# One decoder layer on one core: down projection moved into a Strassen stage of its own, activations through DRAM

## The chip, the core and the metric

The kernel is one program for one core of a Trainium2 chip. Five engines run side by side, each with an instruction queue of its own that it works off in order: PE (TensorE, matrix products), DVE (VectorE), ACT (ScalarE), POOL (GpSimd) and SP (SyncE, which issues nearly all DMAs here). An instruction waits at the head of its queue until the semaphores it names are reached, and everything behind it on that engine waits too. The metric is device time in microseconds (us), the median of the runs shown.

## What is computed

One layer: a mixer, a cross attention over 256 memory tokens, and a feed-forward block, then a final norm, for 1024 tokens of width 1024 in float32. The change lies in the feed-forward block and the norm behind it:

```python
def conv_ffn(h, w_up, conv_w, conv_b, w_down):
    u = h @ w_up                       # 1024 x 1024 @ 1024 x 5632
    u_pad = jnp.pad(u, ((0, 0), (CONV_WIDTH - 1, 0), (0, 0)))
    u = conv_b + conv_w[0] * u_pad[:, 0:s] + conv_w[1] * u_pad[:, 1:1 + s] + conv_w[2] * u_pad[:, 2:2 + s]
    gate = u[..., :D_FF]               # D_FF = 2816
    val = u[..., D_FF:]
    return (jax.nn.silu(gate) * val) @ w_down
...
        x = x + conv_ffn(h, ffn_w_up[l], ffn_conv_w[l], ffn_conv_b[l], ffn_w_down[l])
    return rms_norm(x, norm_final_w)
```

## The kernel before

A float32 value is held as a pair hi + lo, each part in the type float32r (`Pair`). A product of two pairs is three matrix instructions, hi*hi, hi*lo, lo*hi (`mm3`, lines 90 to 92). To make a pair from a plain tile costs one ACT copy that rounds to hi and one DVE subtraction for lo (`split`, lines 96 and 97; for weights `wunit`, lines 117 and 118). "Splitting" a tile below means these two instructions.

The feed-forward block works feature by feature: 22 tiles `f` of 128 gate features and the 128 value features that belong to them. The up projection of a tile is cut in 2 x 2 blocks (gate and value columns by halves of k, halves of k by halves of the 1024 tokens) and done with Strassen's seven products in Winograd's form (`up_strassen`), each product 4 k-steps of three matrix instructions of 512 columns: 84 instructions a tile. The sums of weight blocks are made on POOL (lines 919, 920, 925, 929), and the sums of activation blocks once, before the stage (`sums`, `sums3`, with `whole` on POOL at line 801, `less` on DVE at line 805; the results are the tiles `TT[1]` to `TT[4]`). The first two feature tiles (`up_plain`) are done without Strassen, 96 instructions each, since their products need no `TT`. Every product ends in its own PSUM bank, and DVE adds the seven results together (line 948); then come the convolution (`conv`, ACT line 858, DVE lines 859 and 860), SiLU and product (`swiglu`), and the result is split into the pair `gs[f, b]`.

The down projection runs between the up products (`down(part)`): two feature tiles against 512 output columns, for each of 8 token tiles, 6 instructions of 512 columns, and DVE adds the bank to the residual `xres` (line 1020). It is the plain product, 22 x 2 x 8 x 3 = 1056 instructions. The last four feature tiles are done a token tile at a time with the final norm behind each (`down_norm`, line 998 adds, line 299 norms).

The order of the work: `Job`s hold generators that emit a few instructions at a time; `fill` interleaves them with chains of other work. A scheduler then orders each engine's instructions, except those given to `pin`. Weights come as one stream, two units ahead (`Stream`). Buffers decide when loads may start: `big` has 40 slots of 4 KB a partition, `wts` two raw weight buffers (`wraw`) and four split ones (`whi`, `wlo`), `wsum` one more raw buffer and two for sums.

## Time and profile before

| | us |
|---|---|
| three runs | 1334.48, 1337.21, 1338.45 |
| median | 1337.21 |
| span of the profiled execution, first to last instruction | 1335.7 |
| PE busy in it | 1309.3 |
| DVE busy | 935.5 |
| ACT busy | 572.1 |
| POOL busy | 200.8 |

The feed-forward block takes the second half of the span: its first up products start at 634 us and its last ends near 1328 us. The time of the profiled execution is not listed apart from its span; the median lies 1.5 us above the span. A row of the profile that groups instructions names line, engine, operation, what is written and read (`wl<-ws,wh`: the tile `wl` from `ws` and `wh`; names that begin with `p` are PSUM banks), then count, busy time and mean duration.

### The profile page before, as it was taken

What the parts mean: (1) busy time and instruction counts of PE and PEld (TensorE: products, weight loads), DVE (VectorE), ACT (ScalarE), POOL (GpSimd) and SP (SyncE); (2) the same over time, 40 slices, a digit from 0 to 9 for tenths busy, and PEclk for the clock granted to TensorE, in tenths of its full rate; (3) what the DMA queues carried; (4) which work ended last, traced back from release to release, by engine and by line L of the source; (5) the groups of instructions that cost most, each with busy time, mean ns of one, the idle gap of its engine ahead of it and who ended that gap; (6) DMA issues with size and microseconds to landing.
All of it is one profiled execution on the core that took longest, in us unless ns stands there. A gap on an engine that the chain in (4) does not pass through costs nothing.

```text
span 1335.7 us, 17253 instructions
## 1 busy us (share of the span) xinstructions
PE 1309.3 (98%) x6482; PEld 1091.4 (82%) x6482; DVE 935.5 (70%) x1620; ACT 572.1 (43%) x1041; POOL 200.8 (15%) x252
## 2 busy tenths in 40 slices
PE   8999999999999999999889999999999999999997
PEld 7898878988788898989678888888888888888886
DVE  6723775237667554466997988787979788887984
ACT  6536443364445433344352534242433434342542
POOL 2000110001210000021731211202111212112201
PEclk9999999999999999999999999999999999999999
DMA  9333225332332222212112112121212111121122
GB/s 284 139 96 80 78 91 195 95 79 64 96 131 58 64 64 76 84 63 79 32 32 64 48 48 71 40 74 38 63 32 63 48 48 48 49 76 35 33 94 111
DMA packets 125172, 102.29 MB, mean 77 GB/s; under 512 B 3161, under 2 KB 108319, under 8 KB 125088
## 3 DMA queue, kind: packets, MB, share of 16 engines
q1 hardware_dynamic: 124511, 99.35, 24.1%
q0 software_dynamic: 432, 1.57, 0.3%
q8 instruction: 51, 0.84, 0.3%
...
## 4 chain that ended last, share of the span: by engine, by line
PE 87%; DVE 6%; issue 3%; POOL 2%; ACT 1%; DMA 1%; POOLq 0%; SPq 0%; ACTq 0%; DVEq 0%
PE pa L90 21%; PE pa L92 21%; PE pa L91 21%; PE pb L90 6%; PE pb L91 6%; PE pb L92 6%; DVE r L97 2%; PE pb L307 1%; DVE t L805 1%; DVE f L299 1%; DVE wl L118 1%; POOL s L294 1%; PE pb L650 1%; PE pb L760 1%; PE pb L634 1%
## 5 line engine op out<-in xcount | busy, mean ns | idle before, releaser
L117 ACT ACTIVATE wh<-wr 128x512 fp32r<-128x512 f32 (+1 forms) x264 | 166.1, 631 | 360.1 <-PE pa L92 146.4
L92 PE MATMUL pa<-r,wl 128*128 128x512 f32 (+1 forms) x780 | 302.6, 388 | 7.2 <-DVE wl L118 7.2
L90 PE MATMUL pa<-r,wh 128*128 128x512 f32 (+1 forms) x780 | 308.3, 395 | 0.7 <-ACT r L96 0.7
L118 DVE TENSOR_TENSOR wl<-wr,wh 128x512 fp32r<-128x512 f32 (+1 forms) x264 | 195.2, 740 | 158.7 <-ACT wh L117 153.9
L91 PE MATMUL pa<-r,wh 128*128 128x512 f32 (+1 forms) x780 | 302.0, 387 | 2.4 <-DVE r L97 2.4
L90 PE MATMUL pa<-wh,r 128*128 128x512 f32 (+2 forms) x680 | 238.2, 351 | 0.6 <-ACT r L96 0.6
L92 PE MATMUL pa<-wh,r 128*128 128x512 f32 (+2 forms) x680 | 235.9, 347 | 0.3
L91 PE MATMUL pa<-wl,r 128*128 128x512 f32 (+2 forms) x680 | 235.8, 347 | 0.0
L92 PEld LDWEIGHTS pa<-r,wl 128*128 128x128 f32 x780 | 148.5, 190 | 39.9 <-DVE wl L118 8.2
L91 PEld LDWEIGHTS pa<-r,wh 128*128 128x128 f32 x780 | 149.0, 191 | 33.2 <-DVE r L97 2.9
L90 PEld LDWEIGHTS pa<-r,wh 128*128 128x128 f32 x780 | 148.9, 191 | 32.1 <-issue 1.6
L92 PEld LDWEIGHTS pa<-wh,r 128*128 128x128 f32 x680 | 127.9, 188 | 18.4 <-DVE r L97 1.2
L90 PEld LDWEIGHTS pa<-wh,r 128*128 128x128 f32 x680 | 128.0, 188 | 17.4 <-ACT r L96 1.2
L91 PEld LDWEIGHTS pa<-wl,r 128*128 128x128 f32 x680 | 128.0, 188 | 16.5 <-issue 0.2
L91 PE MATMUL pb<-r,wh 128*128 128x512 f32 x228 | 89.9, 394 | 0.0
L90 PE MATMUL pb<-r,wh 128*128 128x512 f32 x228 | 89.8, 394 | 0.0
L92 PE MATMUL pb<-r,wl 128*128 128x512 f32 x228 | 89.6, 393 | 0.0
L96 ACT ACTIVATE r<-t 128x256 fp32r<-128x256 f32 (+1 forms) x92 | 45.6, 517 | 84.2 <-DVE f L1020 33.4
L117 ACT ACTIVATE wh<-ws 128x512 fp32r<-128x512 f32 x80 | 50.4, 631 | 66.0 <-POOL ws L925 27.6
L948 DVE TENSOR_TENSOR t<-pa,t 128x512 f32<-128x512 f32 x92 | 61.8, 684 | 24.1 <-PE pa L92 24.0
L859 DVE SCALAR_TENSOR_TENSOR t<-t,vec,t 128x511 f32<-128x511 f32 x80 | 67.7, 865 | 7.7 <-ACT t L858 7.7
L858 ACT ACTIVATE t<-t,vec 128x512 f32<-128x512 f32 x80 | 63.1, 813 | 17.3 <-DVE t L948 17.3
...
## 6 DMA issues: line engine op xcount, KB each, us to landing
wr<-in_ffn_w_up_dram SPq DMA_DIRECT2D x44, 512.0 KB, 3.7
wr<-in_w_in_dram SPq DMA_DIRECT2D x24, 512.0 KB, 4.0
wr<-in_ffn_w_down_dram SPq DMA_DIRECT2D x22, 512.0 KB, 3.7
f<-in_xattn_wkv_dram SPq DMA_DIRECT2D x16, 512.0 KB, 7.7
f<-in_x_dram SPq DMA_DIRECT2D x16, 512.0 KB, 7.4
wr<-in_w_out_dram SPq DMA_DIRECT2D x16, 512.0 KB, 3.8
wr<-in_xattn_wq_dram SPq DMA_DIRECT2D x16, 512.0 KB, 3.6
wr<-in_xattn_wo_dram SPq DMA_DIRECT2D x16, 512.0 KB, 3.4
```

The source lines that it names most:

```text
L90: nc.tensor.matmul(ps, l.hi, r.hi, start=start, stop=False)
L91: nc.tensor.matmul(ps, l.hi, r.lo, start=False, stop=False)
L92: nc.tensor.matmul(ps, l.lo, r.hi, start=False, stop=stop)
L96: nc.scalar.activation(dst.hi, src, AF.Copy)
L97: nc.vector.tensor_tensor(dst.lo, src, dst.hi.bitcast(F32), ALU.subtract)
L117: ia = nc.scalar.activation(w.hi, src, AF.Copy)
L118: ib = nc.vector.tensor_tensor(w.lo, src, w.hi.bitcast(F32), ALU.subtract)
L294: nc.gpsimd.tensor_tensor(rs, ss, halfneg[:, 0:1], ALU.pow)
L299: nc.vector.scalar_tensor_tensor(y, xt, inv_rms(xt, y), wb, ALU.mult, ALU.mult)
L858: nc.scalar.activation(c, ps, AF.Identity, bias=cb(f), scale=cw(2, f))
L859: nc.vector.scalar_tensor_tensor(c[:, 1:], ps[:, 0:TB - 1], cw(1, f), c[:, 1:], ALU.mult, ALU.add)
L948: nc.vector.tensor_tensor(dst, ps, other, ALU.add)
```

## The change

- **Up projection.** All 22 tiles use the seven products. Two PSUM banks take six of them in turn and the products of one chain accumulate on top of each other, so that ACT copies a bank out between two products (`copy`, `out`) where DVE added before. The convolution covers all 1024 tokens in one piece. For the first three tiles the two products that need only `H3[0]` run ahead (`up_pre`), and `up(f)` loads their weights again and does the other five. `sums3` is part of `sums`.
- **Through DRAM.** The residual (`xres`, eight tiles) is written to DRAM ahead of the stage (`spill`). Each feature tile's result is written to DRAM as plain float32 (`dma(G[f], cg)`) and not split there.
- **Down projection.** It starts behind all up products (`down`). Its operands are cut in 2 x 2 blocks (tokens by halves, features by halves, output columns by halves) and seven products of 11 k-steps are run, in five stages in this order: `units12` (two products), `units65` (two), `units3`, `units7`, `units4`. A product at one k-step is 12 instructions of 512 columns. Both operands of every product are split when they are used, 14 splits a k-step in all, and sums of blocks are made on POOL (`padd`, `psub`) and DVE (`less`). `take` keeps one pair of units ahead of the one in use. Four banks are held by X all the way, four by Z and later Y. The last stage ends with the final norm of tiles 4 to 7.

The core of the diff (what is taken out is in the listing above):

```diff
+    dram = ctx.enter_context(tc.tile_pool(name="dram", bufs=1, space=bass.MemoryType.DRAM))
+    XS = [dram.tile([P, D], F32, name=f"xd{t}", tag=f"xd{t}") for t in range(8)]
+    def spill(t):
+        dma(XS[t], xres[t])
+    for t in range(4):
+        spill(t)
...
         b11 = b11 or whole(H3[0], 0, c0)
...
+        u = t2(512).rearrange("p (k c) -> p k c", k=HK) if b12 is not None else None
+        if u is None:
+            u = b12 = whole(H3[1], 0, c0)
+        else:
+            nc.scalar.activation(u, b12, AF.Copy)
+        less(b11, u, b11)
         TT[1].put(0, HK, c0, P, b11)
         t = whole(H3[1], HK, c0) if b22 is None else t2(512).rearrange("p (k c) -> p k c", k=HK)
...
+        b22 = t if b22 is None else b22
+        less(u, b22, u)
+        TT[3].put(0, HK, c0, P, u)
+        less(t, b22, b11)
         TT[2].put(0, HK, c0, P, t)
         b21 = b21 or whole(H3[0], HK, c0)
         less(b21, b21, t)
         TT[4].put(0, HK, c0, P, b21)
...
+        spill(4 + i)
...
+    NPRE = 3
+    KH = NF // 2
...
+    def mm3c(ps, l, r, start, stop):
+        kw = dict(skip_group_check=True)
+        nc.tensor.matmul(ps, l.hi, r.hi, start=start, stop=False, **kw)
+        nc.tensor.matmul(ps, l.hi, r.lo, start=False, stop=False, **kw)
+        nc.tensor.matmul(ps, l.lo, r.hi, start=False, stop=stop, **kw)
+    def product(ps, B, fresh):
+        w = ws.take()
+        for k in range(HK):
+            mm3c(ps, w[:, k, :], B(k), fresh and k == 0, k == HK - 1)
+            yield 0.7
...
+        head = [u1, lambda: wunit(st[12], HK, P)]
+        tail = [u6, lambda: wunit(st[1], HK, P), u7, u3, lambda: wunit(st[22], HK, P)]
+        return {"pre": head, "post": tail, "all": head + tail}[part]
...
+    def up_pre(f):
         def gen():
...
+            ps = bankU()
+            yield from product(ps, b11, True)
+            sa, ug = f4(2, TB), f4(2, TB)
+            copy(sa[:, 0, :], ps)
+            yield from product(ps, b21, False)
+            copy(ug[:, 0, :], ps)
+            begun[f] = sa, ug
+        return job([up_units(f, "pre")], gen)
+    def conv(u, f):
+        c = f4(2, TB)
+        u, v = (t.rearrange("p b t -> p (b t)") for t in (u, c))
+        nc.scalar.activation(v, u, AF.Identity, bias=cb(f), scale=cw(2, f))
+        nc.vector.scalar_tensor_tensor(v[:, 1:], u[:, 0:T - 1], cw(1, f), v[:, 1:], ALU.mult, ALU.add)
+        nc.vector.scalar_tensor_tensor(v[:, 2:], u[:, 0:T - 2], cw(0, f), v[:, 2:], ALU.mult, ALU.add)
+        return c
+    def up(f):
+        pre = f < NPRE
         def gen():
...
+            x = bankU()
+            if pre:
+                sa, ug = begun.pop(f)
+            else:
+                yield from product(x, b11, True)
+                sa, ug = f4(2, TB), f4(2, TB)
+                copy(sa[:, 0, :], x)
+                z = bankU()
+                yield from product(z, b21, True)
+                add(ug[:, 0, :], z, sa[:, 0, :])
+            def out(dst):
+                if pre:
+                    add(dst, x, sa[:, 0, :])
+                else:
+                    copy(dst, x)
+            yield from product(x, lambda k: TT[2].k(k), pre)
+            out(sa[:, 1, :])
+            y = bankU()
+            yield from product(y, lambda k: TT[1].k(k), True)
+            sb, uv = f4(2, TB), f4(2, TB)
+            copy(sb[:, 1, :], y)
+            yield from product(x, lambda k: TT[3].k(k), False)
+            out(sb[:, 0, :])
+            padd(uv[:, 1, :], sb[:, 0, :], sb[:, 1, :])
+            yield from product(y, b22, False)
+            add(ug[:, 1, :], y, sa[:, 1, :])
+            cg = conv(ug, f)
+            yield from product(x, lambda k: TT[4].k(k), False)
+            out(uv[:, 0, :])
+            cv = conv(uv, NF + f)
+            nc.scalar.activation(cg, cg, AF.Silu)
+            nc.vector.tensor_tensor(cg, cg, cv, ALU.mult)
+            dma(G[f], cg)
+        return job([up_units(f, "post" if pre else "all")], gen)
...
+        def unit(src):
+            w = Pair(wts.tile([P, 512], F32R, tag="whi", name=nm("wh")),
+                     wts.tile([P, 512], F32R, tag="wlo", name=nm("wl")))
+            split(w, src)
+            return w
...
+        def load(k):
+            a1[k], a2[k] = f4(2, TB), f4(2, TB)
+            dma(a1[k], G[k])
+            dma(a2[k], G[KH + k])
...
+        def run(ps, a, b, fresh, k):
+            for t in range(4):
+                mm3c(ps[t], a[:, t * P:(t + 1) * P], b, fresh and k == 0, k == KH - 1)
+                yield 0.7
+        def units12(k):
+            load(k)
+            b11, b21 = wpair(k, 0)
+            yield unit(a1[k][:, 0, :]), unit(b11)
+            yield unit(a2[k][:, 0, :]), unit(b21)
+        def units65(k):
+            g1, g2 = a1[k], a2[k]
+            b11, b12 = wrow(k, 0)
+            b22 = wpair22(k)
+            x = xs[k // 2][:, k % 2, :] if k % 2 else None
+            if x is None:
+                xs[k // 2] = f4(2, TB)
+                x = xs[k // 2][:, 0, :]
+            padd(x, g1[:, 1, :], g2[:, 1, :])
+            less(g1[:, 1, :], g1[:, 0, :], g1[:, 1, :])
+            less(g1[:, 0, :], x, g1[:, 0, :])
+            t1, t2_ = half(), half()
+            psub(t1, b12, b11)
+            psub(t2_, b22, t1)
+            yield unit(g1[:, 0, :]), unit(t2_)
+            yield unit(x), unit(t1)
...
+        def units3(k):
+            g1, g2 = a1[k], a2[k]
+            less(g2[:, 0, :], g2[:, 0, :], g1[:, 0, :])
+            yield unit(g2[:, 0, :]), unit(wpair22(k))
+        def units7(k):
+            g1 = a1[k]
+            b12, b22 = wpair(k, 512)
+            psub(g1[:, 0, :], b22, b12)
+            yield unit(g1[:, 1, :]), unit(g1[:, 0, :])
+        def units4(k):
+            g1, g2 = a1[k], a2[k]
+            b11, b21 = wpair(k, 0)
+            t = half()
+            psub(t, b21, b11)
+            psub(t, t, g1[:, 0, :])
+            yield unit(g2[:, 1, :]), unit(t)
...
+        feed = (u for us in (units12, units65, units3, units7, units4) for k in range(KH) for u in us(k))
+        ready = []
+        def take():
+            while len(ready) < 2:
+                ready.append(next(feed, None))
+            return ready.pop(0)
+        def gen():
+            wb = bcast_row(norm_final_w)
+            X, Z = banks(), banks()
+            for k in range(KH):
+                yield from run(X, *take(), True, k)
+                yield from run(Z, *take(), True, k)
...
+            s1 = []
+            for t in range(4):
+                s1.append(t2(512))
+                copy(s1[t], X[t])
+                add(R[t][:, 0:512], Z[t], R[t][:, 0:512])
+                padd(R[t][:, 0:512], s1[t], R[t][:, 0:512])
+            turn[0] += 4
+            Y = banks()
+            for k in range(KH):
+                yield from run(X, *take(), False, k)
+                yield from run(Y, *take(), True, k)
+            for t in range(4):
+                s = t2(512)
+                copy(s, X[t])
+                padd(R[t][:, 512:], s, R[t][:, 512:])
+                s = t2(512)
+                copy(s, Y[t])
+                padd(R[4 + t][:, 512:], s, R[4 + t][:, 512:])
+            for k in range(KH):
+                yield from run(Y, *take(), False, k)
+            for t in range(4):
+                add(R[t][:, 512:], Y[t], R[t][:, 512:])
+                nc.sync.dma_start(out=out[t * P:(t + 1) * P, :], in_=normed(R[t], wb))
+            for k in range(KH):
+                yield from run(X, *take(), False, k)
+            for t in range(4):
+                s = t2(512)
+                copy(s, X[t])
+                padd(R[4 + t][:, 512:], s, R[4 + t][:, 512:])
+            sq = [sc(2) for _ in range(4)]
+            y = t2(512)
+            for t in range(4):
+                r = R[4 + t][:, 512:]
+                nc.scalar.activation(y, r, AF.Square, scale=1.0 / 32, accum_out=sq[t][:, 1:2])
+                nc.gpsimd.tensor_tensor(r, r, wb[:, 512:], ALU.mult)
+            for k in range(KH - 2):
+                yield from run(X, *take(), False, k)
+            last = [take(), take()]
+            for t in range(4):
+                for i, (a, b) in enumerate(last):
+                    mm3c(X[t], a[:, t * P:(t + 1) * P], b, False, i == 1)
+                    yield 0.7
+                r, s, ss, rs = R[4 + t], t2(512), sc(1), sc(1)
+                lo, hi = r[:, 0:512], r[:, 512:]
+                add(lo, X[t], lo)
+                nc.scalar.activation(s, lo, AF.Square, scale=1.0 / 32, accum_out=sq[t][:, 0:1])
+                nc.vector.tensor_tensor(lo, lo, wb[:, 0:512], ALU.mult)
+                nc.gpsimd.tensor_scalar(ss, sq[t][:, 0:1], sq[t][:, 1:2], EPS, ALU.add, ALU.add)
+                nc.gpsimd.tensor_tensor(rs, ss, halfneg[:, 0:1], ALU.pow)
+                nc.vector.tensor_scalar(lo, lo, rs, None, ALU.mult)
+                nc.scalar.activation(hi, hi, AF.Copy, scale=rs)
+                for q, h, hs in ((nc.sync, lo, slice(0, 512)), (nc.scalar, hi, slice(512, D))):
+                    q.dma_start(out=out[(4 + t) * P:(5 + t) * P, hs], in_=h)
...
+    for f in range(NPRE):
+        up_pre(f)
+    for f in range(NF):
+        up(f)
...
+    fill_pre(100.0)
     for j in list(plan):
         finish(j)
+    upp.close()
+    dsum = ctx.enter_context(tc.tile_pool(name="dsum", bufs=4))
+    J["down"] = job([], down())
+    finish(J["down"])
```

What stands where the up projection meets its first `TT` operand, on PE (names: `r` are parts of activation operands, `wh` and `wl` those of weights, `pa`, `pb` banks). Before, at the end of the first tile's products for the first half of the tokens:

```order
L91 MATMUL pa_6155<-r_5525,wh_6126 128x512
L92 MATMUL pa_6155<-r_5521,wl_6127 128x512
L90 MATMUL pa_6155<-r_5521,wh_6126 128x512
L91 MATMUL pa_6155<-r_5525,wh_6126 128x512
L92 MATMUL pa_6155<-r_5521,wl_6127 128x512
L90 MATMUL pa_6301<-r_5861,wh_6112 128x512
L91 MATMUL pa_6301<-r_5863,wh_6112 128x512
L92 MATMUL pa_6301<-r_5861,wl_6113 128x512
```

After, near the end of the products that run ahead (the bank that gets its first row here, `pa_6450`, is that of the product with `TT[1]`):

```order
L877 MATMUL pb_6324<-r_5519,wl_6203 128x512
L875 MATMUL pb_6324<-r_5519,wh_6202 128x512
L876 MATMUL pb_6324<-r_5523,wh_6202 128x512
L877 MATMUL pb_6324<-r_5519,wl_6203 128x512
L875 MATMUL pa_6450<-r_6209,wh_6384 128x512
L875 MATMUL pb_6324<-r_5520,wh_6281 128x512
L876 MATMUL pb_6324<-r_5524,wh_6281 128x512
L877 MATMUL pb_6324<-r_5520,wl_6282 128x512
```

In the old order the next 48 rows take the second half of the tokens (`r_5861`, `r_5863`), tile of tokens by tile of tokens; in the new one the next products read `TT[1]` and `TT[2]`, which are sums over all four tiles of tokens of both halves.

What POOL does in the middle of the feed-forward block. Before (`ws` are sums of weight blocks, `wr` raw weights; four rows a feature tile):

```order
L919 TENSOR_TENSOR ws_8855<-wr_8853 128x512
L920 TENSOR_TENSOR ws_8856<-ws_8855,wr_8847 128x512
L929 TENSOR_TENSOR ws_8856<-wr_8847,ws_8856 128x512
L925 TENSOR_TENSOR ws_8965<-wr_8847,wr_8853 128x512
L919 TENSOR_TENSOR ws_9059<-wr_9057 128x512
L920 TENSOR_TENSOR ws_9060<-ws_9059,wr_9031 128x512
L929 TENSOR_TENSOR ws_9060<-wr_9031,ws_9060 128x512
L925 TENSOR_TENSOR ws_9141<-wr_9031,wr_9057 128x512
```

After, in the stage `units65` (`ds` are the half buffers of `dsum`, two rows a k-step):

```order
L1025 TENSOR_TENSOR ds_10237<-ds_10230,ds_10236 128x512
L1025 TENSOR_TENSOR ds_10287<-wr_10280 128x512
L1025 TENSOR_TENSOR ds_10288<-ds_10282,ds_10287 128x512
L1025 TENSOR_TENSOR ds_10339<-wr_10331 128x512
L1025 TENSOR_TENSOR ds_10340<-ds_10333,ds_10339 128x512
L1025 TENSOR_TENSOR ds_10390<-wr_10383 128x512
L1025 TENSOR_TENSOR ds_10391<-ds_10385,ds_10390 128x512
L1025 TENSOR_TENSOR ds_10442<-wr_10434 128x512
```

The rows have the same shape, 128 x 512; they were four for 84 matrix instructions of up and some 48 of down, and are now two for 24 in this stage.

What DVE does at the end of the block. Before, in `down_norm` (`f_2013`, `f_2015` are residual tiles):

```order
L118 TENSOR_TENSOR r_11476<-wr_11471,r_11476 128x512
L998 TENSOR_TENSOR f_2013<-pa_11479,f_2013 128x512
L998 TENSOR_TENSOR f_2013<-pb_11493,f_2013 128x512
L998 TENSOR_TENSOR f_2015<-pb_11515,f_2015 128x512
L299 SCALAR_TENSOR_TENSOR f_11507<-f_2013,s_11509,f_11449 128x1024
L998 TENSOR_TENSOR f_2015<-pb_11529,f_2015 128x512
```

After, from the last splits of `units3` into `units7` (`wl` are the low parts of the units, `f_10121` and on the residual tiles 0 to 3):

```order
L97 TENSOR_TENSOR wl_10948<-f_10044,wh_10947 128x512
L97 TENSOR_TENSOR wl_10954<-ds_10951,wh_10953 128x512
L97 TENSOR_TENSOR wl_10973<-f_9595,wh_10972 128x512
L97 TENSOR_TENSOR wl_10977<-f_9595,wh_10976 128x512
L865 TENSOR_TENSOR f_10121<-pa_10153,f_10121 128x512
L865 TENSOR_TENSOR f_10123<-pa_10154,f_10123 128x512
L865 TENSOR_TENSOR f_10125<-pa_10155,f_10125 128x512
L865 TENSOR_TENSOR f_10127<-pb_10156,f_10127 128x512
L299 SCALAR_TENSOR_TENSOR f_10993<-f_10121,s_10995,f_9585 128x1024
L299 SCALAR_TENSOR_TENSOR f_11002<-f_10123,s_11004,f_9585 128x1024
L97 TENSOR_TENSOR wl_11032<-f_9629,wh_11031 128x512
L299 SCALAR_TENSOR_TENSOR f_11011<-f_10125,s_11013,f_9585 128x1024
```

The four norms (line 299) stand between the low parts that the first and the second k-step of `units7` need (`wl_10977` and `wl_11032`, `wl_11036`), where before they stood behind the additions of a token tile and no split followed them.

## Rows read from the trace of the kernel before

**Rows 1.** The page, parts 1, 2 and 4: busy time, clock, chain of waits

```profile
PE 1309.3 (98%) x6482; PEld 1091.4 (82%) x6482; DVE 935.5 (70%) x1620; ACT 572.1 (43%) x1041; POOL 200.8 (15%) x252
...
PEclk9999999999999999999999999999999999999999
...
PE 87%; DVE 6%; issue 3%; POOL 2%; ACT 1%; DMA 1%; POOLq 0%; SPq 0%; ACTq 0%; DVEq 0%
```

**Rows 2.** Busy time by stretch; columns are named in the first row

```profile
core 0: us, PE busy (x) PEld busy (x) DVE busy (x) ACT busy (x) POOL busy (x), PEclk, DMA share, GB/s
645.00:700.00 55.00, 45.70 (x175) 35.82 (x174) 53.55 (x85) 26.27 (x58) 30.43 (x32) 0.91 0.07 20
900.00:1000.00 100.00, 100.00 (x434) 81.13 (x433) 79.72 (x131) 33.83 (x53) 19.41 (x15) 1.00 0.16 48
```

**Rows 3.** Timeline of PE, feed-forward block begins; start us, duration us, instruction

```profile
633.32 1.04 PE L307 MATMUL pb<-ident,f 128*128 128x128 f32 x8
...
646.15 0.40 PE L90 MATMUL pa<-r,wh 128*128 128x512 f32 x1
649.00 0.53 PE L91 MATMUL pa<-r,wh 128*128 128x512 f32 x1 [2.45 <-DVE r L97]
...
650.18 0.63 PE L91 MATMUL pa<-r,wh 128*128 128x512 f32 x1
...
652.74 0.41 PE L91 MATMUL pa<-r,wh 128*128 128x512 f32 x1
```

**Rows 4.** Timeline of DVE around one POOL instruction

```profile
763.33 0.68 DVE L948 TENSOR_TENSOR t<-pb,t 128x512 f32<-128x512 f32 x1
763.93 1.28 DVE L97 TENSOR_TENSOR r<-t,r 128x512 fp32r<-128x512 f32 x1
...
766.93 0.67 DVE L97 TENSOR_TENSOR r<-t,r 128x512 fp32r<-128x512 f32 x1
```

**Rows 5.** Timeline of POOL, the same stretch

```profile
763.35 1.30 POOL L919 TENSOR_TENSOR ws<-wr 128x512 f32<-128x512 f32 x1 [3.94 <-DVE wl L118]
```

**Rows 6.** Timeline of DVE, ahead of the Strassen products

```profile
636.83 1.75 DVE L299 SCALAR_TENSOR_TENSOR f<-f,s,f 128x1024 f32<-128x1024 f32 x1 [1.20 <-POOL s L294]
...
671.35 2.37 DVE L805 TENSOR_TENSOR t<-t,t 128x512 f32<-128x512 f32 x2
```

**Rows 7.** Timeline of POOL, the same stretch

```profile
670.90 6.32 POOL L801 TENSOR_TENSOR t<-r,r 128x256 f32<-128x256 f32 x6 [0.36 <-DVE r L97]
```

**Rows 8.** Durations of line 801 on POOL: least, median, most

```profile
L801 POOL TENSOR_TENSOR t<-r,r x44: 718/920/1718, 596.9 to 676.3; 128x256 f32<-128x256 f32 x44
```

**Rows 9.** Groups by line and shape: count, busy us, mean ns, idle before

```profile
L117 ACT ACTIVATE wh<-ws 128x512 fp32r<-128x512 f32 x80 | 50.4, 631 | 66.0 <-POOL ws L925 27.6 <-PE pa L91 16.1 <-PE pb L91 10.9
...
L299 DVE SCALAR_TENSOR_TENSOR f<-f,s,f 128x1024 f32<-128x1024 f32 x31 | 41.7, 1346 | 28.1 <-POOL s L294 28.1
...
L118 DVE TENSOR_TENSOR wl<-ws,wh 128x512 fp32r<-128x512 f32 x80 | 54.5, 682 | 17.9 <-ACT wh L117 17.9
L97 DVE TENSOR_TENSOR r<-pb,r 128x256 fp32r<-128x256 f32 x96 | 37.8, 418 | 9.0 <-ACT r L96 8.3
...
L925 POOL TENSOR_TENSOR ws<-wr,wr 128x512 f32<-128x512 f32 x20 | 25.9, 1293 | 138.7 <-DVE wl L118 95.6 <-DVE s L856 43.1
...
L952 ACT ACTIVATE t<-pa 128x512 f32<-128x512 f32 x11 | 6.5, 591 | 7.9 <-DVE t L860 7.9
...
L683 ACT ACTIVATE f<-f 128x1024 f32<-128x1024 f32 x4 | 4.2, 1059 | 0.1
```

**Rows 10.** Busy time by stretch, where DMA moved most

```profile
200.00:210.00 10.00, 10.00 (x49) 8.21 (x48) 5.74 (x12) 3.57 (x9) 0.00 (x0) 1.00 0.99 386
```

**Rows 11.** DMA issues: size, time to landing

```profile
wr<-in_ffn_w_up_dram SPq DMA_DIRECT2D x44, 512.0 KB, 3.7
```

**Rows 12.** Chain that ended last, its end: start, duration, what

```profile
1328.57 0.61 DVE f L998
...
1331.50 0.72 ACT f L1008
```

More of the change, by code (lines that the diff above doesn't have):

```diff
@@ L818, in sums @@
         TT[4].put(0, HK, c0, P, b21)
-    def sums3(i):
-        c0 = i * P
-        b12, b22 = whole(H3[1], 0, c0), whole(H3[1], HK, c0)
-        less(b22, b22, b12)
-        TT[3].put(0, HK, c0, P, b22)
     plan[0].open = True
@@ L898, in strassen_units @@
[L898 to L907 removed]
+    G = [dram.tile([P, 2, TB], F32, name=f"gd{f}", tag=f"gd{f}") for f in range(NF)]
@@ L1012, in down @@
-    def down(part):
-        def gen():
-            for half in range(2):
-                u = [ws.take(0), ws.take()]
-                for t in range(8):
-                    ps = bankU()
-                    yield from down_mm(ps, part * FP, t, u)
-                    xr = xres[t][:, half * 512:(half + 1) * 512]
-                    nc.vector.tensor_tensor(xr, ps, xr, ALU.add)
-        return [rows(w_down, part * FP, FP, half * 512, 512) for half in range(2)], gen
-    plain = [up_plain(f) for f in range(NPLAIN)]
@@ L1024, in hybrid_layer @@
-    up_strassen(2, down(0))
-    up_strassen(3)
-    for part in range(1, NF // FP - 2):
-        up_strassen(2 * part + 2)
-        job(*down(part))
-        up_strassen(2 * part + 3)
-    for f in range(NF - 2, NF):
-        up_strassen(f)
-    job([rows(w_down, k0, FP, half * 512, 512, k0 == NF - FP) for k0 in (NF - 2 * FP, NF - FP) for half in range(2)],
-        down_norm)
+        head = [u1, lambda: wunit(st[12], HK, P)]
+        tail = [u6, lambda: wunit(st[1], HK, P), u7, u3, lambda: wunit(st[22], HK, P)]
```

207 lines of the change are left out of this document (65 added, 142 removed).

## The prediction

> **What bounds the kernel now.** I read the page first: PE is busy for 98% of the span, its granted clock is full almost throughout, and the chain that ended last is 87% PE [rows 1]. The busy times by stretch say where that holds. Inside the feed-forward block PE is busy 100.00 of 100 us and starts 434 matrix instructions, one every 0.2304 us; DVE is at 80%, POOL at 19%, DMA at 48 GB/s [rows 2]. So the block is as long as its instructions of 512 columns, and removing one saves 0.2304 us as long as nothing else becomes late. The one soft place is the block's start, 645 to 700 us: PE is busy 45.70 of 55 us there and the clock is 0.91 of full [rows 2], because DVE still makes the operands (the 2.45 us before the instruction at 649.00, put down to DVE, is one of the waits). After that wait the instructions from 650.18 to 652.74 stand 0.427 us apart, the lower of the two clock levels [rows 3]. Such a wait costs its length and some eight instructions by 0.2 us, 1.6 us more. The stretch loses 9.3 us idle and 0.09 x 55 = 5.0 us to the clock, 14.3 in all.
>
> **What the change removes.** Up: 2 tiles at 96 and 20 at 84 are 1872 instructions; 22 at 84 are 1848. Down: 1056 become 7 x 11 x 12 = 924. That is 156 fewer, 156 x 0.2304 = -35.9 us.
>
> **What two engines can do at once.** The new stage gives DVE and POOL the work of the splits and sums, so their joint pace is the question. While POOL's 128 x 512 sum ran from 763.35 to 764.65, the DVE subtraction queued at 763.93 took 1.28 us where the same one takes 0.67 at 766.93; the addition that reads a PSUM bank, started at 763.33, took its usual 0.68 [rows 4, 5]. DVE instructions with both inputs in SBUF and POOL sums exclude each other. In the next pattern both queues are full: two subtractions took 2.37 us together, six POOL sums of 256 elements 6.32 [rows 6, 7]; a DVE one costs 0.60 start to start [rows 4], so each POOL sum held DVE up by about 0.57, although alone it shows 0.72 [rows 8]. About 0.16 of a POOL instruction therefore lies beside DVE. For 512 elements, 1.29 alone [rows 9], I take 1.12 us beside a DVE of 0.61. The bounds are 0.6, the wait actually seen at 763.93, if POOL falls into DVE's gaps, and 1.29 + 0.68, nothing overlapped.
>
> The Trainium skill says in "SBUF — State Buffer", section "Who interferes with whom", that such a pair locks the shared read port for the full instruction, the loser blocking fully. The trace agrees on who blocks, and differs on how long: the cycle above is shorter than the sum of both durations. By the rule taken to the letter the two stages below that are bound by this would be 14 us longer together, and the time 1371.
>
> **The change part by part**, in us against the present loss:
>
> *Start of the block: +7 (2 to 12).* PE begins the up products at 633.3 [rows 3]. The 72 instructions that run ahead, 16.6 us, and two groups of eight transposes, some 0.8 us each, last to 651.5. What comes next reads `TT[1]` of all four token tiles. DVE's last norm starts at 636.83 and ends at 638.6 [rows 6]; in the new order 26 subtractions of 256 elements (0.34: 0.42 [rows 9] less the 0.08 by which neighbours overlap), 17 of 512 and on POOL 18 sums of 256 and 3 of 512 stand between it and that operand: 8.8 + 10.4 + 18 x 0.57 + 3.4 = 32.9, so 671. PE stands some 19.5 us and loses 1.7 to the clock, 21 against the 14.3 of now.
>
> *Up products: 0.* 84 instructions are 19.35 us a tile. DVE has 7 low parts, 2 additions, 4 convolution passes and a product of 1024 (1.2 each): 11.5; POOL 5 x 1.12 = 5.6. Their 17 us fit. A bank is written again 12 instructions (2.76 us) after its copy can start; on ACT a split (0.63) and the copy (0.59) [rows 9] stand before that. Units are split three products ahead, so a late one is covered.
>
> *Start of the down stage: +8.5 (4 to 11).* Behind the last up product DVE still has the second half of the gate's convolution, two passes for the values, the product, then two low parts: about 4.3 x 1.3 [rows 9] + 2 x 0.68 = 7. PE has only four hi*hi instructions that it can start earlier (-0.9); the clock takes 1.7; ACT's SiLU (1.06 [rows 9]) adds to the chain, 0.7.
>
> *Stage units12: +1 (0 to 4).* Its 1.57 MB a k-step in 5.53 us are 284 GB/s; DMA has moved 386 [rows 10]. DVE has 4 low parts, 2.4 us.
>
> *Stage units65: +15 (0 to 24).* PE needs 11 x 5.53 = 60.8. Between its first and last k-step DVE has 69 instructions on SBUF and POOL 27: 42.1 + 30.2 = 72.3, +11.5. At its start POOL works off seven sums on the residual and operands before the second k-step's `psub`; I add 3.5 for that.
>
> *Stage units3: +5 (0 to 8).* Both engines together: 22 x 0.61 + 15 x 1.12 = 30.2, PE 30.4. But seven bank copies, 7 x 0.59 = 4.1, stand on ACT before the second k-step's hi parts.
>
> *Stage units7: +8 (1 to 10).* The four norms stand on DVE before the low parts of the second k-step. Each waits for its square on ACT (1.06) and is 1.3 long [rows 9]: addition, square, two small POOL steps, four norms and two low parts are ready 10.3 us after the stage begins; PE wants them after 2.76.
>
> *Stage units4: +10 (0 to 14).* 22 low parts and 22 POOL sums: 13.4 + 24.6 = 38.0 against 30.4, +7.6; four copies and four squares on ACT among the splits add some 2.4.
>
> *End: +1.5 (0 to 4).* Now the last addition starts at 1328.57 and the last ACT instruction at 1331.50 [rows 12]. The new end has the same steps, with two token tiles' work mixed, and four tiles to write instead of one.
>
> *DRAM.* 11.5 MB written and read again and 4 MB of residual are hidden by the same 386 GB/s. The G write waits on SP for its tile, with the raw weights of two tiles on ahead of it.
>
> Sum: 7 + 8.5 + 1 + 15 + 5 + 8 + 10 + 1.5 = 56; 56 - 35.9 = +20.1. The profiled execution would go from 1335.7 to 1355.8; the median lies 1.5 above the span, so **1357 us**.
>
> **The rivals.**
> 1. *The splits and sums stay beneath PE.* If POOL falls into DVE's gaps (0.6 a piece), units65 needs 42.1 + 16.2 = 58 < 60.8 and units4 26.6 < 30.4. Then the start, the stage's start and the end remain, 7 + 8.5 + 1.5 = 17: 1337.2 - 35.9 + 17 = 1318. For it: over the 33 us of units12 nothing competes, and the scheduler already puts ten of POOL's sums there. Against it: [rows 6, 7], two full queues.
> 2. *PE falls to its lower clock and stays there.* From units65 to units4 there are 660 instructions; at 0.427 [rows 3] each costs 0.197 more. If half of them do, 65 us, of which waits of 38 are replaced: 1384 and up; all, 1449. I put it at 1395. For it: after the one wait shown the clock is low. Against: waits of a microsecond, the kind expected here, are not what stands before it.
>    The Trainium skill, "TensorE: Matmul & The Clock Gate", section "A second HAM failure mode: psum-queue depth-cycling", describes frequent small idle gaps between groups as enough for the clock to swing. The trace shows only the longer wait; that rule speaks for this rival.
> 3. *Loads bind units12.* Two raw buffers: if three loads of 3.7 us [rows 11] land one after another, a k-step is 11.1 and nine of them cost 50 more: 1407. The operand loads have free slots, so only one of the three waits for a buffer.
> 4. *The accumulation does not hide.* If the copies out of the banks come 0.5 us late, five a tile, 22 x 5 x 0.5 = 55: 1412, and PE would fall below 99% in the up stage.
>
> **How the numbers follow.** Forecast 0.60 (its own range 1335 to 1380), rival 1 0.20, rival 2 0.10, rivals 3 and 4 0.05 each. About 0.3% can be told from no change, 1333 to 1341: that takes 0.06 out of the forecast and 0.01 out of rival 1. Faster 0.20, same 0.07, slower 0.73. Range 1318 to 1392: half of rival 1 lies below, rivals 3, 4 and half of 2 above. The low end also holds the sum of the low bounds of the middle stages.
>
> **What would show it.** In the profile after: about 156 fewer rows on PE and the same spacing of 0.23 us where it is busy; PE idle for 15 to 22 us before the first product with `TT[1]`; PE at 99% or more through the up products; 5 to 9 us idle before the first down product; then PE busy 75 to 85% in units65 and units4 with DVE and POOL together full, and one wait of 5 to 8 us early in units7. If POOL sums there show 1.3 us and DVE subtractions 0.68 throughout, the joint pace is wrong and rival 1 holds. If PE is 100% busy from the first to the last down product, the forecast is wrong as a whole.

## The result and the profile after

The changed kernel takes 1385.27 us (median of four runs, 1385.08 to 1385.43) against 1336.33 for the kernel before (median of four: the three runs listed ahead, and one of 1335.44): 1.0368 times as long, 95% interval 1.0353 to 1.0383. It is slower, as forecast, but by 48.9 us where 20 were forecast. The profiled execution has a span of 1382.5 us, 46.8 above the span before; the steps below account for the spans. The other 2.1 us of the difference of the medians are not traced to a step.

The page of the changed kernel, parts 1, 2 and 5 (columns as in [rows 1] and [rows 9]):

```profile
span 1382.5 us, 17155 instructions
PE 1295.0 (94%) x6326; PEld 1066.4 (77%) x6326; DVE 881.8 (64%) x1247; ACT 644.3 (47%) x1157; POOL 393.7 (28%) x352
...
L97 DVE TENSOR_TENSOR wl<-f,wh 128x512 fp32r<-128x512 f32 x88 | 78.6, 904 | 75.4 <-ACT wh L96 75.4
```

PE has 156 instructions fewer, as counted; POOL's busy time is twice that of [rows 1]; the DVE subtraction that makes a low part of 128 x 512 takes 904 ns in the mean in the down stage, where such a one took 682 in [rows 9].

From here on, "instruction" without an engine is a matrix instruction of 512 columns on PE. What a stage loses is its length less 0.2304 us for each instruction that starts in it. Busy time by stage; the stretches run from the first instruction of a stage to that of the next: the first 240 up instructions, the other up instructions, the gap, then `units12`, `units65`, `units3`, `units7`, `units4` and the end (columns as in [rows 2]):

```profile
631.62:717.44 85.82, 63.93 (x252) 49.25 (x250) 73.25 (x99) 38.34 (x78) 47.55 (x39) 0.88 0.24 74
717.44:1089.01 371.57, 371.57 (x1609) 301.72 (x1607) 260.97 (x267) 195.29 (x283) 150.25 (x96) 1.00 0.27 87
1089.01:1094.44 5.43, 0.39 (x3) 0.00 (x1) 5.36 (x4) 3.99 (x6) 2.17 (x1) 0.94 0.04 17
1094.44:1160.57 66.13, 64.31 (x265) 51.14 (x265) 38.29 (x54) 27.40 (x49) 6.18 (x4) 0.95 0.85 308
1160.57:1247.91 87.34, 67.43 (x266) 50.25 (x264) 69.05 (x76) 27.70 (x49) 53.92 (x38) 0.92 0.39 122
1247.91:1290.36 42.45, 35.74 (x134) 26.70 (x132) 24.85 (x23) 14.64 (x26) 31.99 (x21) 0.88 0.56 181
1290.36:1330.63 40.27, 32.98 (x134) 25.72 (x132) 22.29 (x31) 18.31 (x34) 8.62 (x11) 0.92 0.17 66
1330.63:1370.53 39.90, 35.26 (x132) 26.12 (x131) 30.54 (x24) 15.79 (x34) 34.79 (x24) 0.91 0.21 66
1370.53:1382.47 11.94, 0.39 (x2) 0.00 (x0) 4.46 (x8) 4.22 (x8) 4.91 (x7) 0.63 0.47 176
```

The kernel before loses 16.0 us in the first 240 instructions of the block, and has 8.3 from its last one to the end. Its other 2687 lose 2.9. Against that, and beside the forecast:

| step | forecast (bounds) | measured | how |
|---|---|---|---|
| start of the block | +7 (2 to 12) | +12.0 | 85.82 - 240 x 0.2304 = 30.5; less 16.0, less 2.5 because PE begins 2.5 us earlier |
| up products | 0 | -1.5 | loses 1.3, where the rest of the block lost 2.9 |
| start of the down stage | +8.5 (4 to 11) | +8.8 | 5.2 in the gap, 3.6 in the first k-step |
| units12, the rest | +1 (0 to 4) | +1.7 | 5.3 less those 3.6 |
| units65 | +15 (0 to 24) | +26.5 | 87.34 - 264 x 0.2304 |
| units3 | +5 (0 to 8) | +12.0 | 42.45 - 132 x 0.2304 |
| units7 | +8 (1 to 10) | +9.9 | 40.27 - 30.41 |
| units4 | +10 (0 to 14) | +9.7 | 39.90 - 131 x 0.2304 |
| end | +1.5 (0 to 4) | +3.6 | 11.9 against 8.3 |
| sum | 56 | 82.7 | less 35.9 for the instructions: +46.8, the difference of the two spans |

The up products, the start of the down stage, `units12`, `units7` and `units4` come within 2 us of their forecast; 11.5 of the 27 us missing stand in `units65`, 7 in `units3`, 5 at the start of the block, 2 at the end and 2 in `units7`.

In `units65` the loss is of two kinds. Its first three groups of 12 instructions (a group is one product at one k-step) lose 17.2 us, 11.57 of them in one wait. Eight of the next ten groups lose 8.2 together, the others next to nothing. The wait on PE (start, duration, instruction):

```profile
1180.11 0.79 PE L875 MATMUL pb<-wh,wh 128*128 128x512 f32 x1 [11.57 <-ACT wh L96]
```

The hi part that it waits for is made from a weight difference on POOL. POOL, between the sums of the first k-step and those of the second (`f<-f,f` are the sums x that `units65` makes, one a k-step, `f<-t,f` those onto the residual, `ds` the weight differences):

```profile
1154.31 1.29 POOL L1025 TENSOR_TENSOR ds<-wr 128x512 f32<-128x512 f32 x1 [63.13 <-DMA wr<-in_ffn_w_down_dram]
1155.68 1.62 POOL L1025 TENSOR_TENSOR ds<-ds,ds 128x512 f32<-128x512 f32 x1
1157.26 9.80 POOL L868 TENSOR_TENSOR f<-f,f 128x512 f32<-128x512 f32 x6
1167.01 3.41 POOL L868 TENSOR_TENSOR f<-t,f 128x512 f32<-128x512 f32 x2
1170.38 1.70 POOL L868 TENSOR_TENSOR f<-f,f 128x512 f32<-128x512 f32 x1
1172.05 1.26 POOL L868 TENSOR_TENSOR f<-t,f 128x512 f32<-128x512 f32 x1
1173.26 1.26 POOL L868 TENSOR_TENSOR f<-f,f 128x512 f32<-128x512 f32 x1
1174.48 1.26 POOL L868 TENSOR_TENSOR f<-t,f 128x512 f32<-128x512 f32 x1
1175.70 1.26 POOL L1025 TENSOR_TENSOR ds<-wr 128x512 f32<-128x512 f32 x1
1176.92 1.26 POOL L868 TENSOR_TENSOR f<-f,f 128x512 f32<-128x512 f32 x1
1178.14 1.26 POOL L1025 TENSOR_TENSOR ds<-ds,ds 128x512 f32<-128x512 f32 x1
```

DVE, the same stretch:

```profile
1165.83 1.77 DVE L813 TENSOR_TENSOR f<-f 128x512 f32<-128x512 f32 x1
1167.52 1.77 DVE L97 TENSOR_TENSOR wl<-f,wh 128x512 fp32r<-128x512 f32 x1
1169.22 1.74 DVE L813 TENSOR_TENSOR f<-f,f 128x512 f32<-128x512 f32 x1
1180.09 1.20 DVE L97 TENSOR_TENSOR wl<-ds,wh 128x512 fp32r<-128x512 f32 x1 [9.13 <-ACT wh L96]
...
1185.19 0.68 DVE L97 TENSOR_TENSOR wl<-ds,wh 128x512 fp32r<-128x512 f32 x1
```

While both queues are full, one DVE and one POOL instruction together take 1.70 us (POOL starts at 1167.01, with 3.41 for the next two; DVE at 1165.83, 1167.52, 1169.22). From 1171.0 to 1180.1 DVE's queue holds nothing that may run, and from 1172.05 on a POOL sum takes 1.22 from start to start; at 1185.19 DVE alone takes 0.68. So the joint price that the prediction took, 1.12 + 0.61 = 1.73, holds. What stands ahead of the due weight difference is another thing: nine sums x, all those still to come up to the last k-step, four residual sums and the difference that it is made from, from 1157.26 to 1178.14.

The first of the POOL rows shows where those sums could have gone. POOL stood still for 63.13 us, nearly all of `units12`, because the first weight difference of `units65` was at the head of its queue and waited for its load; the nine sums x stood behind it, and the loads of what they add had all been issued by 1135.8. No run put them ahead of that difference.

The second kind of loss, in the later groups, is the joint pace and not the time that results take from engine to engine: DVE never stands idle there.

```profile
1185.80:1220.50 34.70, 28.84 (x116) 20.93 (x115) 34.70 (x44) 11.52 (x20) 13.96 (x9) 1.00 0.38 114
```

In `units3` the wait stands behind POOL too. POOL, then ACT, then PE, around its second k-step:

```profile
1252.80 1.26 POOL L1025 TENSOR_TENSOR f<-wr 128x512 f32<-128x512 f32 x1 [2.00 <-DMA wr<-in_ffn_w_down_dram]
1254.02 8.82 POOL L868 TENSOR_TENSOR f<-t,f 128x512 f32<-128x512 f32 x6
```

```profile
1255.31 0.60 ACT L871 ACTIVATE t<-pb 128x512 f32<-128x512 f32 x1 [5.38 <-POOL f L868]
1255.80 0.62 ACT L96 ACTIVATE wh<-f 128x512 fp32r<-128x512 f32 x1
```

```profile
1255.96 0.80 PE L875 MATMUL pb<-wh,wh 128*128 128x512 f32 x1 [5.62 <-ACT t L871]
```

A weight difference for `units7`, a stage ahead, waits for its load; behind it on POOL stands the residual sum that frees a buffer of `tmp` (the pool of six buffers that the copies write to), on which the last bank copy on ACT waits 5.38 us, and behind that copy the hi part that PE needs.

### The profile page after: what moved, and what is told of

It is laid out like the page before. It is cut to its first block, busy times and chain, and to the rows that moved or that the text cites. A ratio compares the mean times of both kernels' runs of the same rounds, so it can differ in the third digit from the quotient of the medians.

```text
span 1382.5 us, 17155 instructions
## 1 busy us (share of the span) xinstructions
PE 1295.0 (94%) x6326; PEld 1066.4 (77%) x6326; DVE 881.8 (64%) x1247; ACT 644.3 (47%) x1157; POOL 393.7 (28%) x352
## 3 DMA queue, kind: packets, MB, share of 16 engines
q10 hardware_dynamic: 576, 1.05, 0.2%
## 5 line engine op out<-in xcount | busy, mean ns | idle before, releaser
L90 PE MATMUL pa<-wh,r 128*128 128x512 f32 (+2 forms) x480 | 159.1, 332 | 0.0
L92 PE MATMUL pa<-wh,r 128*128 128x512 f32 (+2 forms) x480 | 157.1, 327 | 0.2
L91 PE MATMUL pa<-wl,r 128*128 128x512 f32 (+2 forms) x480 | 157.2, 328 | 0.0
L875 PE MATMUL pa<-r,wh 128*128 128x512 f32 x384 | 152.3, 397 | 3.8 <-DVE f L865 3.8
L877 PE MATMUL pa<-r,wl 128*128 128x512 f32 x384 | 151.3, 394 | 0.0
L876 PE MATMUL pa<-r,wh 128*128 128x512 f32 x384 | 151.3, 394 | 0.0
L90 PE MATMUL pa<-r,wh 128*128 128x512 f32 (+1 forms) x384 | 149.2, 389 | 0.7 <-ACT r L96 0.7
L92 PE MATMUL pa<-r,wl 128*128 128x512 f32 (+1 forms) x384 | 144.2, 375 | 0.3 <-DVE wl L118 0.3
L91 PE MATMUL pa<-r,wh 128*128 128x512 f32 (+1 forms) x384 | 144.0, 375 | 0.3 <-DVE r L97 0.3
L97 DVE TENSOR_TENSOR wl<-f,wh 128x512 fp32r<-128x512 f32 x88 | 78.6, 904 | 75.4 <-ACT wh L96 75.4
L92 PEld LDWEIGHTS pa<-wh,r 128*128 128x128 f32 x480 | 90.3, 188 | 9.4 <-DVE r L97 1.0
L90 PEld LDWEIGHTS pa<-wh,r 128*128 128x128 f32 x480 | 90.4, 188 | 7.8 <-ACT r L96 0.2
L954 DVE SCALAR_TENSOR_TENSOR f<-f,vec,f 128x1023 f32<-128x1023 f32 x44 | 83.7, 1903 | 15.8 <-ACT f L953 15.8
L875 PEld LDWEIGHTS pa<-r,wh 128*128 128x128 f32 x384 | 72.4, 189 | 21.1 <-ACT f L871 3.0
L117 ACT ACTIVATE wh<-ws 128x512 fp32r<-128x512 f32 x88 | 55.3, 629 | 67.4 <-PE pa L876 35.9
```

Of the source, the lines that this page charges most:

```text
L90: nc.tensor.matmul(ps, l.hi, r.hi, start=start, stop=False)
L91: nc.tensor.matmul(ps, l.hi, r.lo, start=False, stop=False)
L92: nc.tensor.matmul(ps, l.lo, r.hi, start=False, stop=stop)
L97: nc.vector.tensor_tensor(dst.lo, src, dst.hi.bitcast(F32), ALU.subtract)
L117: ia = nc.scalar.activation(w.hi, src, AF.Copy)
L875: nc.tensor.matmul(ps, l.hi, r.hi, start=start, stop=False, **kw)
```

## The experiments

Ten kernels, each timed beside the kernel before, which took 1336.4 to 1336.5 us in every set. The first three tell apart what holds the down stage: A, what a POOL sum costs beside DVE; B, only the order on POOL; C, the loads. The fourth asks what PE lacks at the block's start: a free bank (D), or work (E).

**1. The operand sums of the down stage on DVE.**

```diff
-            nc.gpsimd.tensor_tensor(dst, a, b, ALU.subtract)     # psub
+            nc.vector.tensor_tensor(dst, a, b, ALU.subtract)
-            padd(x, g1[:, 1, :], g2[:, 1, :])
+            add(x, g1[:, 1, :], g2[:, 1, :])
```

> Edit: the operand sums of the down stage (padd of x and both kinds of psub) go from POOL to DVE; the sums onto the residual stay on POOL. Changed kernel: 1385.3 us. Theory A (a POOL sum and a DVE instruction with both inputs in SBUF exclude each other, so a POOL sum costs the pair 1.1 us where a DVE one costs 0.61): units65 has 96 DVE instructions on SBUF, 58.6 us, below PE's 60.8, so the 11.4 us that its later k-steps lose now go; the wait before its second k-step (13.4) shrinks to about 4, because 14 sums of 1.2 to 1.7 us no longer stand in one queue; units3 and units4 lose about 11 less. Sum about -31: 1354 (1345 to 1362). Theory B (only the order on POOL matters, not what a sum costs): the wait before the second k-step goes, the pace of units65 stays at 3.5 to 4.1 us a product-step because DVE now has more to do: about 1372. Theory C (the loads behind two raw buffers set the pace): within 5 us of 1385.

Measured: 1359.16 us, ratio to before 1.0173 (1.0156 to 1.0190). `units65`, `units3` and `units4` in its trace:

```profile
1159.45:1224.32 64.87, 61.95 (x265) 49.36 (x264) 64.41 (x99) 27.52 (x49) 8.44 (x6) 1.00 0.47 148
1224.32:1266.88 42.56, 34.02 (x133) 26.48 (x132) 31.57 (x41) 14.32 (x26) 10.33 (x7) 0.92 0.60 181
1307.33:1346.55 39.22, 34.27 (x132) 26.55 (x131) 32.18 (x38) 15.95 (x34) 13.29 (x10) 0.91 0.21 67
```

`units65` loses 4.0 instead of 26.5 us, with 99 DVE instructions where it had 76 and 6 on POOL where it had 38: DVE's busy time falls from 69.05 to 64.41 although it does more. That is A; B and C are out for this stage. The 11 us that I expected in `units3` and `units4` did not come (losses 12.2 and 9.0): the residual sums stayed on POOL. Experiments 2 and 5 show that these hold `units3`, and `units4` for the larger part.

**2. X and Y added by DVE out of the banks.**

```diff
-                copy(s, X[t])
-                padd(R[t][:, 512:], s, R[t][:, 512:])
+                add(R[t][:, 512:], X[t], R[t][:, 512:])
```

(and so at the other three places)

> Edit: X and Y are added to the residual by DVE straight out of the banks; the 16 ACT copies and the 16 POOL sums behind them are gone, the operand sums stay on POOL. Theory A: the second k-step of units65 waits 4 POOL sums (some 6.8 us) less, the first wait of units3 (6.7, an ACT copy that waits for a buffer that a POOL sum frees) goes, with 3.5 of the clock and of late low parts behind it, and units4 loses some 4 less at its first k-steps; the pace of units65 stays. About -19: 1366. Theory B (the operand sums are ordered too far ahead, and that alone makes the waits): only units3 gains, about -7: 1378. Theory C: no change.

Measured: 1370.17, ratio 1.0265 (1.0244 to 1.0286). Here `units65`, `units3`, `units4`:

```profile
1161.22:1245.19 83.97, 68.30 (x265) 50.08 (x264) 71.80 (x83) 26.58 (x46) 48.20 (x32) 0.96 0.43 132
1245.19:1279.34 34.15, 32.01 (x133) 24.56 (x133) 24.04 (x26) 11.54 (x20) 19.44 (x14) 1.00 0.67 217
1319.13:1355.30 36.17, 32.83 (x133) 23.84 (x132) 34.06 (x27) 15.11 (x32) 29.66 (x20) 1.00 0.22 73
```

`units3` loses 3.7 for 12.0 and `units4` 6.0 for 9.7, as A has it. `units65` gains only 3.4, half of what A had for four sums less in its wait; its operand sums stay.

**3. The same sums on POOL, in their written order.**

```diff
-            nc.gpsimd.tensor_tensor(dst, a, b, ALU.subtract)     # psub; padd likewise
+            pin(nc.gpsimd.tensor_tensor(dst, a, b, ALU.subtract))
```

> Edit: nothing is added or removed; POOL keeps the written order of its sums in the down stage, so that the sums x of later k-steps no longer run ahead of the weight sums of the second. Theory B (the order on POOL makes the waits): the 13.4 us before the second k-step of units65 shrink to under 3 and the 6.7 in units3 go: about -15, 1370. Theory A (the joint pace of POOL and DVE): what was done during the wait must now be done later at 1.1 us a sum beside a full DVE, so that units65 loses about as much as now, spread over its k-steps; only units3 gains, some 6: 1379 (1372 to 1385).

Measured: 1389.31, ratio 1.0400 (1.0384 to 1.0415): 4 slower than the changed kernel, outside both ranges and against B. `units65` now loses 30.7 (10.8 in its first three groups, the rest spread over the others, most of which take 3.5 to 4.6 us instead of 2.77). So that the sums x ran ahead had not been the cost in itself: done in their own k-steps, they cost as much beside a full DVE. `units3` gains 7.6 as expected, but `units4` loses 17.8 instead of 9.7, because four residual sums and four products with the norm's weights come in one block, 10.3 us from 1326.93, ahead of its second weight difference.

**4. Five feature tiles run ahead instead of three.**

```diff
-    NPRE = 3
+    NPRE = 5
```

> Edit: NPRE 5 for 3: the two products that need only H3[0] run ahead for five feature tiles, 48 instructions (11.1 us) more that need no TT. In the changed kernel PE stands 9.4 and 6.4 us before 671 with 36 of its 72 such instructions still undone. Theory D (the bank copies on ACT stand behind hi parts of TT that wait for POOL and DVE, so that PE has work and no bank): 3 us or less of gain, 1383 or worse. Theory E (TT is late and PE has nothing else): 11 us more of work lies in the wait, -10: 1375.

Measured: 1391.92, ratio 1.0419 (1.0403 to 1.0434), 6.6 more than the changed kernel: D's side. What decides is the trace of the changed kernel, where PE stands still with 36 of its 72 instructions left. PE, then ACT, there:

```profile
651.92 0.80 PE L875 MATMUL pb<-r,wh 128*128 128x512 f32 x1 [9.43 <-ACT f L871]
```

```profile
649.74 1.64 ACT L96 ACTIVATE r<-t 128x256 fp32r<-128x256 f32 x5 [3.20 <-DVE t L813]
651.29 0.57 ACT L871 ACTIVATE f<-pb 128x512 f32<-128x512 f32 x1
```

The copy that PE waits for stands on ACT behind five hi parts, which wait for DVE's differences. More products ahead only add copies to that queue; the first 240 instructions lose 26.6, 4 less. And a tile run ahead costs later: the waits of PE from 690 us on in this experiment,

```profile
PE pb L875 <- DVE f L865: 3.8, 2, 2.6
PE pa L875 <- DVE f L865: 3.7, 2, 2.5
```

are for the additions (L865) that such a tile has in place of copies, on DVE behind the passes of the convolution; the up instructions behind the first 240 lose 11.5 instead of 1.3.

**5. Experiments 1 and 2 together.**

> Edit: both earlier edits together: operand sums of the down stage on DVE, and X and Y added to the residual by DVE straight out of the banks. POOL has no 512-wide sum left in the down stage but the four products with the norm's weights. Theory A: units65 stays at the 4 us of loss that it has with DVE sums, units3 goes from 12.2 to about 3.5, units4 (22 low parts, 22 differences, 8 additions, 4.9 x 0.61 over 30.4) from 9.0 to about 3, units7 stays at 10: 1359.2 - 8.7 - 6 = 1344.5. Rival F (DVE is now the full engine and each thing moved to it costs as much as it saves): units4 keeps its 9 and units65 gets 3 more: about 1354.

Measured: 1341.53, ratio 1.0040 (1.0025 to 1.0055). `units65` to `units4`:

```profile
1161.26:1224.99 63.73, 62.52 (x265) 48.99 (x264) 63.15 (x105) 25.58 (x45) 0.00 (x0) 1.00 0.47 147
1224.99:1256.28 31.29, 31.28 (x134) 24.57 (x133) 24.65 (x41) 12.71 (x23) 0.00 (x0) 1.00 0.60 186
1256.28:1296.02 39.74, 33.76 (x133) 26.52 (x132) 29.76 (x44) 16.98 (x31) 6.27 (x8) 0.91 0.44 151
1296.02:1329.80 33.78, 31.16 (x133) 24.31 (x132) 29.11 (x41) 15.07 (x32) 7.57 (x6) 1.00 0.26 79
```

With POOL at 0.00 in the first two, they lose 2.9 and 0.9; `units4` 3.6; `units7` still 9.3. Together the edits bring 43.7 us, more than one by one (26.1 and 15.1): F is out.

**6. That, and the norms of `units7` spread over its k-steps.**

```diff
-                nc.sync.dma_start(out=out[t * P:(t + 1) * P, :], in_=normed(R[t], wb))
             for k in range(KH):
                 yield from run(X, *take(), False, k)
+                if k in (2, 4, 6, 8):
+                    t = k // 2 - 1
+                    nc.sync.dma_start(out=out[t * P:(t + 1) * P, :], in_=normed(R[t], wb))
```

> Edit: the kernel with both edits, and the four norms of units7 are emitted behind its k-steps 2, 4, 6 and 8 instead of all ahead of the stage. Theory G (the low parts of the second k-step stand behind four norms on DVE, each of which waits for its square on ACT): the 7.8 us before the second k-step and some 1 of the clock go: 8 less than the kernel with both edits, about 1336. Rival H (a norm stalls DVE wherever it stands, since each waits 2 to 3 us for square and POOL steps): four waits of about 1.5 remain with 1.6 of the clock each, a gain of 3 or none: 1341 to 1345.

Measured: 1335.55, ratio 0.9995 (0.9985 to 1.0004); 6.0 less than experiment 5. `units7` loses 2.6 instead of 9.3, in pieces of under a microsecond; 0.7 came back in `units4`. G, at three quarters of its price. What DVE did in the changed kernel, and the wait of PE behind it:

```profile
1298.12 1.29 DVE L299 SCALAR_TENSOR_TENSOR f<-f,s,f 128x1024 f32<-128x1024 f32 x1 [0.44 <-POOL s L294]
1300.12 1.28 DVE L299 SCALAR_TENSOR_TENSOR f<-f,s,f 128x1024 f32<-128x1024 f32 x1 [0.71 <-POOL s L294]
1301.33 1.89 DVE L97 TENSOR_TENSOR wl<-f,wh 128x512 fp32r<-128x512 f32 x3
```

```profile
1302.07 0.80 PE L876 MATMUL pb<-wl,wh 128*128 128x512 f32 x1 [5.90 <-DVE wl L97]
```

The low parts of the later pairs stood behind these norms, each of which waits for its own sum of squares.

**7. Two plain tiles at the start, nothing run ahead.** The only edit to the changed kernel:

```diff
-    NPRE = 3
+    NPRE = 0
+    NPLAIN = 2
...
+    def up_plain(f):                       # 4 x 24 instructions, banks copied out by ACT
...
+    for f in range(NPLAIN):
+        up_plain(f)
```

> Edit: one part undone: the first two feature tiles are done without Strassen again (96 instructions each, 24 more in all, 5.5 us), and no products run ahead; the rest as in the changed kernel. Theory E (PE has nothing else to do until TT is there at 671): 192 instructions, 44 us, need no TT, so the start loses about 16 us as in the kernel before, not 30.5; less 5.5 for the instructions and with the late additions of the three tiles (6.7) gone: about 1372. Theory D (bank copies on ACT stand behind hi parts): eight banks take the eight products, so nothing waits for a copy at first; the same 1372. Rival I (what the plain tiles put on ACT and DVE delays TT as much as PE gains): 1381 to 1386.

Measured: 1372.94, ratio 1.0281 (1.0264 to 1.0298), 12.3 less than the changed kernel. The first 240 instructions lose 10.8 instead of 30.5:

```profile
633.19:699.27 66.08, 60.01 (x251) 47.79 (x250) 54.97 (x82) 34.45 (x72) 30.86 (x27) 0.95 0.20 64
```

The start's loss came from giving up the plain tiles. D and E both forecast this, so the run does not tell them apart; rival I is out.

**8. The sums ahead of TT on DVE.**

```diff
-            pin(nc.gpsimd.tensor_tensor(r[:, j:j + 2, :], h.hi.bitcast(F32), h.lo.bitcast(F32), ALU.add))
+            nc.vector.tensor_tensor(r[:, j:j + 2, :], h.hi.bitcast(F32), h.lo.bitcast(F32), ALU.add)
```

> Edit: the 256-wide sums ahead of TT (whole) go from POOL to DVE, and their order is the scheduler's. Theory A: a POOL sum of 256 costs the pair 0.57, a DVE one 0.34, so TT is ready about 18 x 0.23 = 4 us earlier: 1381 (1379 to 1383). Rival F (DVE is full at the start and takes the sums on top, because POOL's sums lay in its gaps): TT is 2 to 6 us later: 1387 to 1391.

Measured: 1380.15, ratio 1.0325 (1.0309 to 1.0340), 5.1 less than the changed kernel; the first 240 instructions lose 25.6 for 30.5. That is A's side: F is out. The edit changes the order of these sums too, so that their price alone is the cause is not shown.

**9 and 10. All of 1, 2, 6 and 7; and 8 on top.**

> Edit: DVE sums, additions straight out of the banks, late norms and the two plain tiles together. If the four causes are separate (theories A, E and G), the gains add up: 1335.6 - (1385.3 - 1372.9) = 1323.2, 1% under the kernel before. If the start's gain is swallowed later, because the down stage begins sooner than its loads: 1328 or more.

Measured: 1322.64, ratio 0.9902 (0.9886 to 0.9917): a version that beats both kernels, by 13.9 us under the one before, and the gain of the plain tiles adds to that of the other three edits to within 0.6 us.

> Edit: the same, and the sums ahead of TT on DVE too. With two plain tiles PE has work until TT is there, so an earlier TT is worth little; what is left at the start (10.8 us, of which 9.3 in products 24 to 72 that wait for H3 of the second half) ends sooner only if POOL's sums delay the parts of H3 on DVE. Theory A: 2 to 4 us less, 1320. Rival F: DVE is the full engine there and gets 18 sums more ahead of the parts of H3: 2 to 4 us more, 1326.

Measured: 1329.39, ratio 0.9948 (0.9936 to 0.9961), 6.8 more than experiment 9. It is slower, as F has it, by more than F's 2 to 4 us, and the reason is not quite F's: the waits of experiment 9 at the start (4.05 and 2.26 us, both for copies on ACT) shrink to one of 0.95, and one long one comes in their place. PE, then DVE:

```profile
PE pa L878 <- DVE wl L118: 11.5, 1, 11.5
```

```profile
669.97 1.22 DVE L976 TENSOR_TENSOR f<-f,f 128x1024 f32<-128x1024 f32 x1
671.11 2.50 DVE L118 TENSOR_TENSOR wl<-wr,wh 128x512 fp32r<-128x512 f32 x4
```

The low part of a weight that PE wanted at about 660 stands on DVE behind the first tile's convolution and product and the last parts of TT.

## Why the prediction was wrong

The direction, the terms of the start of the down stage, `units12` and `units7`, and the instruction count held. The forecast fell 28 us short, mostly because of what stood in the queues ahead of due work. These steps failed:

- **Start of `units65`, the term of 3.5.** The prediction put seven sums ahead of the second k-step's `psub`. The trace shows twelve: eight sums x and four on the residual, 18.4 us from 1157.26 to 1175.70, with a ninth x before the last difference. The term measured 17.2, with some ten instructions at the lower clock (0.427 us apart) behind the wait. The pace term (11.5) measured 9.3, the remainder; it had counted the sums x that were already done. The row count was wrong; the price of a pair was right. Experiments 1 and 3 speak for the price: with DVE sums the stage loses 4.0, with another order of the same sums 30.7. An order with the sums x in POOL's 63.13 idle us was not tried, so that no order would have helped is not shown.
- **`units3`, the term of 5.** It took the joint work of DVE and POOL to fit, and seven copies on ACT to cost their own 4.1 us. What was left out is that a copy needs a buffer of `tmp`, that only a residual sum on POOL frees it, and that on POOL a difference for the next stage waits for its load first (2.00 us at 1252.80). Measured 12.0; 3.7 without copies and sums (experiment 2).
- **Start of the block, the term of 7.** Measured 12.0. The forecast had PE do its 72 instructions that run ahead without a wait and then stand 19.5 us for TT, which it put at 671. PE stood twice before that, 9.43 us with 36 of them undone and 6.36 with 24, both times for a copy on ACT that empties a bank. The first row with `TT[1]` began at 668.07, right behind another instruction; the last of the 72 began at 671.55, and for a part of TT PE stood only once, 0.35 us before 673.93. The loss of the first 72 instructions, 23.3 us (39.93 less 72 x 0.2304), is near the 21 forecast, but made of other waits, so the agreement is in part luck. What no term held is the 7.2 us from there to the 240th; 5.5 of them stand at the late additions of the tiles run ahead (waits of 1.19 and 2.57 us for DVE, and some eight slow instructions behind the second). That `up products` cost nothing holds for the other nineteen tiles.
- **`units4`, the term of 10: right by luck.** The forecast had 7.6 for the joint pace and 2.4 for ACT. Of the 9.7 measured, 6.9 stand in the second to fourth group of 12 instructions, where residual sums and products with the norm's weights stand on POOL among the differences; the other groups lose 2.8. Experiment 1, which takes the differences off POOL, gains 0.7 here; experiment 2, which takes the residual sums, 3.7.
- **End.** +3.6 for +1.5; not tested.

The rule of the Trainium skill that the prediction weighed ("SBUF — State Buffer", sections "Terms" and "Who interferes with whom": such a pair contends for a shared port that is locked for the full instruction) gave 1371, nearer the result, but not for its reason: the pair takes 1.70 us, less than the 1.22 + 0.60 that its parts take alone from start to start, so the joint pace that was forecast stands.

Rival 1 (splits and sums beneath PE) was wrong for `units65` and `units4`, the stages that it named. Of the ten POOL sums that it counted on in `units12`, the trace shows two sums x before the stage, and none in it until 1157.26. Rival 2 (the lower clock throughout) was wrong: the clock is at 0.92 in `units65`, and 1.00 in the same stage without POOL's sums. It is 1.00 too from 1185.8 to 1220.5, where PE stands for 0.36 to 1.05 us eight times; small gaps alone did not lower it here. Rival 3 was wrong: `units12` loses 5.3 us with DMA at 308 GB/s. Rival 4, copies on ACT that do not hide, was wrong where it was put, in the up products in general, and right in two places that it did not name, the start and `units3`.

What stays open: why the last stage's end is 2 us longer than forecast, the 8.8 us between up and down, which no experiment touched, and what the order with POOL's idle time used would take.
